# The numerator and denominator products of an mLSTM head, one at a time between the matmuls of the next large product

## The chip, the cores and the metric

One core of a Trainium2 chip runs one launch of the kernel. The metric is the device time of a launch in microseconds, as the median of several runs; before the change it is 1035.16 us, in three runs between 1034.41 and 1039.77.

## What is computed

One step of a decoder layer for T = 560 tokens: 16 meta tokens, 512 prompt tokens and 8 sequences of 4 sample tokens that carry states of their own. The layer is half a SwiGLU FFN, a mixer, and half a second FFN. The mixer sends the normalised input through one matrix `w_in` and gives parts of the result to four mLSTM heads (128 wide) and to an RG-LRU (512 channels). What the change touches is one line pair of an mLSTM head:

```
def mlstm_chunk(q, k, v, ig, logf, C0, n0, m0):
    ...
    s = jnp.einsum('bhtd,bhsd->bhts', q, k) * w_intra
    num = jnp.einsum('bhts,bhse->bhte', s, v) + w_inter[..., None] * jnp.einsum('bhed,bhtd->bhte', C0, q)
    den = jnp.sum(s, axis=-1) + w_inter * jnp.einsum('bhd,bhtd->bht', n0, q)
    h = num / jnp.maximum(jnp.abs(den), jnp.exp(-m))[..., None]
```

The prompt is one sequence and starts from zero states, so `C0` and `n0` matter for the 32 sample tokens alone.

## The kernel before

**Large products.** Weights and inputs of the matrix products are split into a high and a low part (`whi`, `wlo`, `xh`, `xl`), and a product is three passes over these, by `split_mm` (L275). A row block of `w_in` (128 output rows) takes 8 blocks of the inner dimension x 3 passes = 24 pairs of matmuls, each of a pair over half of the tokens (280, or 272 where the meta tokens aren't needed). Weights come by DMA on SP's queue, ScalarE makes the high part (L256) and VectorE the low one (L261), some blocks ahead of the products.

**The mixer's order.** The table `PLAN` (L33) lists every step of the mixer by hand: `k2` is the product of w_in for the keys of head 2, `v1` for the values of head 1, `x`, `y` and `o` for the RG-LRU's input, its output gate and the heads' output gates. TensorE, ScalarE and VectorE each run their instructions in the order in which these steps issue them. GpSimd and SP are placed by the scheduler. A row of `PLAN` begins with a large product, and the steps behind it in the row issue small work that is meant to run under or right after it.

**The steps around the change.** `n` (do_n, L1319) is the change's step: 18 products into PSUM tiles `pn` (two banks) and `pden` (one). Eight are products of `c0` (the sample states) with `qw`, 4 columns each; one is the sample's own `V5`; five are the blocks of V with the causal weights `W` (512, 400, 272, 144 and 16 columns); two small ones add up the sample's denominators; two go into `pden`. All but the last two are in full fp32, and one of those shows as two records in the profile. `cn` (L1341) copies `pn` and `pden` out on ScalarE; `cm` splits squares on ScalarE and VectorE (L1352 to L1355); `f` (L1362) sums these on TensorE; `cf` makes the reciprocal root (`rs` on ScalarE, L1370) and a Newton step on VectorE (`nt`, `rs`, L318 to L320).

`a` and `b` (lru_gate, L1043) are gate products of the RG-LRU, 6 matmuls of 292 columns each into `prg`, from `xch` and `xcl`, the split of the convolved input (`hx`, L1039 and L1040); `ta` and `tb` (L1053) are the tanh that ScalarE takes of them. `ca` and `cb` go on from there. `tv` and `tk` (turn, L1193) turn values and keys on TensorE (`pt`). `ev`, `ey` and others (L857) copy a large product out of PSUM on VectorE, with the norm's factor `r`. `hd` (L1166, L1167) splits `D`, which GpSimd sums from `W`. `p` (L1380) makes the new states, and `cp` adds them into `c0` on VectorE (L1397, `c<-c,px`).

**PSUM.** Large products, `prg`, `pn`, the `px` of step `p` and the `pv` of step `f` take turns in three tiles of two banks each (`mm_tile`). A matmul that opens a tile waits until the last reader of what lay there is done.

Lines are those of the kernel before.

Of the kernel before, what the change touches and what calls it, by code (L numbers as in the profile page):

```python
# [5 lines left out]
F32 = mybir.dt.float32  # L6
# [5 lines left out]
P = 128  # L12
KD = 8            # 1024 / 128
KF = 22           # 2816 / 128
T = 560           # 16 meta + 512 prompt + 8 x 4 sample tokens
C16 = 16
TQ = T - C16      # tokens whose outputs are needed
NP = 528
Q = 280           # half of the tokens
AHEAD = 8, 6, 5, 4          # how far loads, sums and both steps of the split run ahead of the products  # L20
MANUAL = {mybir.EngineType.PE, mybir.EngineType.Activation, mybir.EngineType.DVE}
TCUT = 272        # where the last row blocks are cut
DED = 7           # row blocks of h with a place of their own
PLAIN = 4, 3      # row blocks of h from plain products, in both FFNs
FT = 15           # where the last row blocks of h are cut for w_down
TAIL = 5          # row blocks of x that FFN 2 ends with
NB = 8
# [4 lines left out]
# the mixer, in the order of its steps (see there)  # L32
# [9 lines left out]
v1 sd0 ev1 hq1 L1 hx1 cb0 hd0 qw0 vm0 n0 a1 cc0 sk0 b1 cd0 cn0 ta1 cm0 tb1  # L42
k2 ca1 cb1 ek2 cc1 tv1 am1
x2 f0 cv1 p0 ex2 cf0 tk1 cp0 cx2 ck1
q2 L2 s1 w1 m1 sd1 eq2 hx2 hq2
v2 ev2 cd1 hd1 a2 ta2 ca2 b2 cb2 vm1 sk1 qw1 tb2 n1 cc2 cn1 hk2 ce0
x3 cm1 ex3 f1 cf1 ce1 am2
k3 w2 tv2 cx3
q3 cv2 ek3 hx3 eq3 p1 s2 tk2 cd2 cp1 ck2
v3 qw2 m2 vm2 L3 a3 sd2 hd2 ev3 n2 ta3 ca3 b3 hk3 cb3 cn2 tv3 tb3 cc3 sk2 am3 cd3  # L50
o0 p2 hq3 cv3 cm2 ce2 ce3 w3 eo0
y0 cp2 qw3 to0 ln lr ey0 gy0
o1 eo1 mo0 s3 my0 m3 f2 sd3
y1 tk3 cf2 to1 hd3 ey1 gy1 ck3 so0 mo1 n3 sk3 cn3 cm3
y2 ey2 so1 f3
o2 my1 cf3 gy2 sy0 vm3
# [11 lines left out]
IN = [t for t in PLAN if t == "g" or t[0] in "kqvoxy" and t[1].isdigit()]       # row blocks of w_in  # L68
OUT = (4, 5, 6, 7, 0, 1, 2, 3)                                   # rows of w_out
# [5 lines left out]
# the beginnings of both FFNs, in the order of their steps (see `ffn`)  # L75
# [10 lines left out]
# columns of the constant array  # L86
G1, GM, G2, GF = 0, 8, 16, 24
CW = 32           # [ct, 4]
# [6 lines left out]
CS = 72           # [ct, b, 3]  # L95
H0 = 168          # [ct, b]
N0 = 200          # [h, b]
NCONST = 232

# Products of h with w_down (see `ffn`): of its second part, and under them the first part is made in quarters,  # L100
# with their sums; then the seven products of every pair of row blocks, and between them some of the others.
# [15 lines left out]
# The seven products: weights, right side, bank, and whether they open it. After one, what its bank holds goes  # L117
# into a quarter of the result.
# [6 lines left out]
# packed columns of the causal weights of one head, by block of keys  # L125
WO = (0, 512, 912, 1184, 1328, 1344)
WTOT = 1376
T0 = (16, 128, 256, 384, 512)      # first query of each block of keys
KROWS = (128, 128, 128, 128, 16, 32)

# columns of the output array of small states
# [5 lines left out]
def hymba_step(ctx, tc, xT, wgu1, wdn1, win, wout, wgu2, wdn2, consts, small, c0t, wrg,  # L137
# [11 lines left out]
    # ---------------------------------------------------------------- weights  # L149
    # Products take their weights in the order of this list, 512 columns at a time: blocks of w, or  # L150
    # quarters and sums of quarters of [gate, up] (see ups7). Loads and splits run ahead of them.
# [19 lines left out]
    def blocks(ff):  # L171
        """Row blocks of h: the plain ones, those that go through w_down by seven products, the others, and these
        in two parts."""
        a, b = PLAIN[ff], PLAIN[ff] + 8
        return (0, a), (a, b), {"d": (b, KF), "e": (b, FT), "t": (FT, KF)}
# [30 lines left out]
    state = {"use": 0}  # L206
# [22 lines left out]
    def quarter_sum(q, k):  # L229
        """s1 = w21 + w22, s2 = s1 - w11, s3 = w11 - w21, s4 = w12 - s2, the last in place of s2."""  # L230
        if k in q:
            return
        q[k] = q["s2"] if k == "s4" else sp.tile([P, 512], F32, tag="s", name=k, bufs=4)
        x, y, op = {"s1": ("21", "22", ALU.add), "s2": ("s1", "11", ALU.subtract),
                    "s3": ("11", "21", ALU.subtract), "s4": ("12", "s2", ALU.subtract)}[k]
        dve.tensor_tensor(q[k], q[x], q[y], op=op)  # L236

    def sums(i):
# [3 lines left out]
        b = units[i - 1 - AHEAD[1] + AHEAD[3]]           # s2 is split by now  # L242
# [32 lines left out]
    def split_mm(ps, ks, xh, xl, c0, first=True, last=True, hfs=(0, 1), w=None):  # L275
        """ps += w.T @ x[k] over the k of ks, in three passes of split operands."""
        n = (T - c0) // 2
        for j, k in enumerate(ks):
# [5 lines left out]
            for i, (a, b) in enumerate(((wh, xh), (wh, xl), (wl, xh))):  # L284
                for hf in hfs:
                    state["mm"] = pe.matmul(ps[:, hf, :n], a[:, ws], b[k][:, c0 + hf * n:c0 + hf * n + n],  # L286
                                            start=first and j == 0 and i == 0,
                                            stop=last and j == len(ks) - 1 and i == 2)

# [9 lines left out]
    # -------------------------------------------------------------- constants  # L299
# [16 lines left out]
    def newton(r, v, t, c=0.0):  # L316
        """One Newton step of r towards 1/sqrt(v + c)."""
# [4 lines left out]
    def rsqrt(r, v, t):  # L322
        """r = 1/sqrt(v + eps): the table's value and a Newton step."""
# [9 lines left out]
    def ars(_=0):  # L333
        """Loads the table of 1/sqrt before it is needed."""
        act.activation(dum, eps_c, AF.Abs_reciprocal_sqrt, bias=eps_c, scale=0.0)

    class Norm:
        """Splits x*g for the products and gathers the mean square beside them."""
# [49 lines left out]
    # -------------------------------------------------------------------- FFN  # L388
    # Seven products (Strassen's, in Winograd's form) of quarters of weights x quarters of a right side
    # (halves of its rows x halves of the tokens), for two row blocks of the result at a time. The last two  # L390
    # products of a pair lie behind the first of the next.
# [12 lines left out]
    def ups7(fs, c0, zs, h, xs):  # L404
        """Row blocks of silu(gate) * up: as they are where zs has a place for them, else split into h."""
# [50 lines left out]
    def down7(c0, xs):  # L456
        """Steps of the products for row blocks d and d + 4 of what the first part of h adds to x."""
# [19 lines left out]
    def h_tiles(hp, a, b, x0):  # L477
        """Tiles of h from a to b: where x was, from slot x0, and then in this pool."""
# [16 lines left out]
    def ffn(ff, nrm, c0, hp, plan, mid, steps):  # L495
        """The first row blocks come from plain products, of x * g, and go through w_down at once; under them
        the normalised x is made in quarters (halves of the rows, halves of the tokens), with the sums of
        quarters that the seven products take. down(c, h): the products of the other chunks with w_down."""
# [106 lines left out]
    # ------------------------------------------------------- FFN 1, from DRAM  # L605
# [55 lines left out]
    def start_add(d):         # on two engines: 0 to 4, 5 to 7, and both  # L661
# [5 lines left out]
    def start_warm():         # nothing reads it: the clock of the products wakes up  # L667
# [7 lines left out]
    with tc.tile_pool(name="hp1", bufs=1) as hp, tc.tile_pool(name="sp1", bufs=1) as sp:  # L675
# [9 lines left out]
        def lru_consts():  # L685
            """softplus(-lambda) = max(-lambda, 0) + log1p(exp(-|lambda|)), and halves of what goes into tanh."""
# [12 lines left out]
    # ------------------------------------------------------------------ mixer  # L699
# [4 lines left out]
    # ------------------------------------------------- FFN 2 and the last norm  # L704
    with tc.tile_pool(name="hp2", bufs=1) as hp, tc.tile_pool(name="sp2", bufs=1) as sp:
# [4 lines left out]
        def out_square(d, a, b):  # L710
            """Squares of the tokens from a to b; x becomes x*g."""
# [23 lines left out]
        # the last row blocks in two pieces of tokens, so that the first goes out under the second  # L735
# [32 lines left out]
def mixer(ctx, tc, e):  # L768
# [23 lines left out]
    # ------------------------------------------------------------- constants  # L792
# [4 lines left out]
    cmask = mp.tile([P, P], F32, name="cmask")           # 0 where t >= s  # L797
# [3 lines left out]
    smask = mp.tile([32, NB, 4], F32, name="smask")      # same sequence and t >= s  # L801
# [5 lines left out]
    seqm = mp.tile([96, NB], F32, name="seqm")           # 1 where the row is of sequence b  # L807
# [7 lines left out]
    keep = row("keep")                                   # 0 where a sequence or a block starts  # L815
# [21 lines left out]
    # -------------------------------------------------------------- products  # L837
# [24 lines left out]
    # ----------------------------------------------------------------- gates  # L862
    # Their 8 columns stand beside the rest of their split, so that two passes do.
# [21 lines left out]
    def do_ga(_):             # ig and the forget gate's, with biases  # L885
# [17 lines left out]
    def seq(ap, j):           # column j of every sample sequence  # L903
# [26 lines left out]
    rows = dp.tile([3, H, TQ], F32, name="rows")         # of every head, to be read back on every partition  # L930
# [17 lines left out]
    # Rows to be columns: Bc at 0 (own blocks of keys), the states' weights at 32, at 64 the sums to the next  # L948
    # block and three times the sample's weights, at 96 those to the blocks after it and the sample's Bc.
# [23 lines left out]
    wst = mp.tile([P, 6, H], F32, name="wst")            # weights of the states: 4 blocks, tail, sample  # L973
# [10 lines left out]
    def do_gq(_):  # L984
# [7 lines left out]
        wsp = mp.tile([96, H], F32R, name="wsp")         # split: hi, hi, lo  # L992
# [5 lines left out]
    def bias(i, j, h):  # L998
        """Of the keys of block i for the queries of block j; 4: tail, 5: sample."""
# [535 lines left out]
```

## Time and profile before

| | |
|---|---|
| median of the runs | 1035.16 us |
| profiled execution: span from first to last instruction | 1033.8 us |
| profiled execution: a time of its own beside the span | none is given |
| TensorE busy | 1012.8 us |
| VectorE, ScalarE, GpSimd busy | 834.7, 559.9, 124.0 us |
| DMA | 99.57 MB, a mean of 96 GB/s |
| mean granted TensorE clock | 0.989 of full speed |

A row of the timeline gives the start, the length in microseconds, the engine, the line, the operation, what it writes and reads, and how many instructions were drawn together; in brackets stands how long the engine was idle before it, and who released it. A row of the waits gives who waited for whom, the total, the count and the longest. A row by windows gives a stretch and its length, then the busy time (and count) of TensorE, its weight loads, VectorE, ScalarE and GpSimd, then the granted clock, the DMA engines' share and GB/s.

### The profile page before, as it was taken

Reading aid. Unit: us, or ns where it says so; the run is one execution under the profiler, and the core shown is the slowest. Engines: PE = TensorE matmul, PEld = TensorE weight load, DVE = VectorE, ACT = ScalarE, POOL = GpSimd, SP = SyncE. Lnnn points to the kernel's source line nnn. Section 1 sums busy time; section 2 is a strip of 40 time slices with the busy share of each in tenths; the row PEclk is TensorE's granted clock in tenths of the full one; section 3 lists DMA queues with packets and bytes.
Section 4 is the critical chain, followed back from the end, with each engine's and each line's share of the span. In section 5 each row is a group of like instructions: output and inputs, shape, how many; then the busy total and the mean of one; then the engine's idle time right before and its main releaser. Section 6 shows DMA issues by size and latency. Waiting matters only on the chain.

```text
span 1033.8 us, 20127 instructions
## 1 busy us (share of the span) xinstructions
PE 1012.8 (98%) x7782; PEld 996.4 (96%) x7782; DVE 834.7 (81%) x1448; ACT 559.9 (54%) x1070; POOL 124.0 (12%) x185
## 2 busy tenths in 40 slices
PE   7999999999999999999999999999999999999995
PEld 7999999999999999989999999999999999999995
DVE  7889888888778797888868775789888889859774
ACT  5544555566554455466756643554555566644542
POOL 2000000000000034444443101100000000000114
PEclk9999999999999999999999999999999999999998
DMA  6322322322332334223132123122332323233222
GB/s 215 103 83 72 110 86 101 104 93 96 101 100 64 92 109 143 86 79 127 48 120 85 62 92 119 58 67 101 103 103 95 110 93 112 92 102 93 82 65 87
DMA packets 57479, 99.57 MB, mean 96 GB/s; under 512 B 7840, under 2 KB 14624, under 8 KB 57384
## 3 DMA queue, kind: packets, MB, share of 16 engines
q1 hardware_dynamic: 57384, 98.30, 29.1%
q8 instruction: 61, 1.00, 0.4%
q14 instruction: 34, 0.28, 0.1%
HBM read 93.57 MB, written 4.70 MB: 95 GB/s over the span
## 4 chain that ended last, share of the span: by engine, by line
PE 86%; DVE 7%; issue 2%; ACT 1%; POOL 1%; DMA 1%; SPq 0%; POOLq 0%; DVEq 0%; ACTq 0%
PE pb L397 26%; PE pad L397 20%; PE pd L286 15%; PE po L286 7%; PE pu L286 4%; PE pg L286 4%; PE pv L286 2%; PE py L286 2%; DVE wlo L261 1%; PE pn L1328 1%; PE pd L753 1%; PE p L286 1%; PE px L286 1%; PE pk L286 1%; PE pn L1324 0%
## 5 line engine op out<-in xcount | busy, mean ns | idle before, releaser
L256 ACT CAST whi<-raw 128x512 fp32r<-128x512 f32 (+2 forms) x289 | 173.6, 608 | 176.0 <-PE pad L397 41.1
L261 DVE TENSOR_TENSOR wlo<-raw,whi 128x512 fp32r<-128x512 f32 (+2 forms) x289 | 197.1, 699 | 69.3 <-ACT whi L256 68.9
L256 ACT CAST whi<-s 128x512 fp32r<-128x512 f32 x180 | 112.1, 623 | 105.8 <-PE pb L397 36.4
L261 DVE TENSOR_TENSOR wlo<-s,whi 128x512 fp32r<-128x512 f32 x180 | 124.2, 691 | 12.8 <-ACT whi L256 6.5
L397 PE MATMUL pad<-q21h,whi 128*128 128x280 f32 (+1 forms) x360 | 104.2, 289 | 0.9 <-ACT whi L256 0.9
L397 PE MATMUL pb<-qt4l,whi 128*128 128x280 f32 (+1 forms) x360 | 104.0, 289 | 0.0
L397 PE MATMUL pad<-q21l,whi 128*128 128x280 f32 (+1 forms) x360 | 104.0, 289 | 0.0
L397 PE MATMUL pad<-q21h,wlo 128*128 128x280 f32 (+1 forms) x360 | 104.0, 289 | 0.0
L397 PE MATMUL pb<-qt4h,whi 128*128 128x280 f32 (+1 forms) x360 | 103.9, 289 | 0.0
L397 PE MATMUL pb<-qt4h,wlo 128*128 128x280 f32 (+1 forms) x360 | 103.9, 289 | 0.0
L366 POOL TENSOR_TENSOR acc<-acc,sq 128x560 f32<-128x560 f32 (+1 forms) x12 | 18.1, 1512 | 435.1 <-ACT sq L365 434.8
L397 PEld LDWEIGHTS pad<-q21h,whi 128*128 128x128 f32 x360 | 67.8, 188 | 1.1 <-ACT whi L256 1.1
L397 PEld LDWEIGHTS pb<-qt4h,whi 128*128 128x128 f32 x360 | 67.9, 189 | 0.0
L397 PEld LDWEIGHTS pb<-qt4h,wlo 128*128 128x128 f32 x360 | 67.8, 188 | 0.0
L397 PEld LDWEIGHTS pad<-q21l,whi 128*128 128x128 f32 x360 | 67.8, 188 | 0.0
L397 PEld LDWEIGHTS pb<-qt4l,whi 128*128 128x128 f32 x360 | 67.8, 188 | 0.0
L397 PEld LDWEIGHTS pad<-q21h,wlo 128*128 128x128 f32 x360 | 67.8, 188 | 0.0
L236 DVE TENSOR_TENSOR s<-raw 128x512 f32<-128x512 f32 x90 | 61.5, 683 | 1.7 <-DMA raw<-in_wdn 1.7
L286 PE MATMUL pd<-hl,whi 128*128 128x280 f32 (+1 forms) x294 | 61.6, 291 | 0.8 <-DVE hl L529 0.8
L286 PE MATMUL pd<-hh,whi 128*128 128x280 f32 (+1 forms) x294 | 61.3, 290 | 0.8 <-ACT hh L526 0.8
L286 PE MATMUL pd<-hh,wlo 128*128 128x280 f32 (+1 forms) x294 | 61.3, 289 | 0.0
L721 POOL TENSOR_TENSOR acc<-acc,sq 128x272 f32<-128x272 f32 x12 | 11.4, 969 | 350.4 <-ACT sq L717 350.4
(457 smaller groups left out, 3029.0 us busy)
## 6 DMA issues: line engine op xcount, KB each, us to landing
raw<-in_wgu SPq DMA_DIRECT2D x174, 256.0 KB, 2.7
raw<-in_wdn SPq DMA_DIRECT2D x71, 256.0 KB, 2.8
raw<-in_win SPq DMA_DIRECT2D x50, 256.0 KB, 2.8
raw<-in_wout SPq DMA_DIRECT2D x16, 256.0 KB, 2.7
raw<-in_wdn SPq DMA_DIRECT2D x18, 192.0 KB, 2.4
out_y<-X SPq DMA_DIRECT2D x4, 544.0 KB, 3.1
c<-in_c0t SPq DMA_DIRECT2D x4, 512.0 KB, 3.6
out_o_cs<-c SPq DMA_DIRECT2D x4, 512.0 KB, 3.9
```

Of the source, the lines that this page charges most:

```text
L236: dve.tensor_tensor(q[k], q[x], q[y], op=op)
L256: act.copy(ready[i][0][:, :src.shape[-1]], src)
L261: dve.tensor_tensor(lo, src, hi, op=ALU.subtract)
L286: state["mm"] = pe.matmul(ps[:, hf, :n], a[:, ws], b[k][:, c0 + hf * n:c0 + hf * n + n], start=first and j == 0 and i == 0, stop=last and ...
L366: (dve if d == KD - 1 else pool).tensor_tensor(self.acc[:, c0:], self.acc[:, c0:], s[:, c0:], op=ALU.add)
L397: pe.matmul(ps, a[:, k * P:k * P + P], b, start=first and k == 0 and i == 0, stop=k == KD // 2 - 1 and i == 2, skip_group_check=not first)
L721: pool.tensor_tensor(acc[:, a:b], acc[:, a:b], s[:, :b - a], op=ALU.add)
L753: pe.matmul(ps, u[:, i % 4 * P:i % 4 * P + P], v[:, C16 + a:C16 + b], start=i == 0 and m == 0, stop=f == c1 - 1 and m == 2)
L1328: pe.matmul(pn[:, 0, a:512], V[:KROWS[i], i, :P], W[:KROWS[i], WO[i]:WO[i] + 512 - a], start=i == 0, stop=i == 4)
```

## The change

`do_n` no longer issues its products. It appends 18 closures to a list. `split_mm` calls `fill()` after every pair of matmuls, which takes one closure from the list and issues it. A new step `nz`, directly behind the large product, issues what is left (nothing, as 18 is less than 24). Inside a head's group the order is new: each block of V is followed by two products of `c0`, then V5 and the rest.

```
-    state = {"use": 0}
+    state = {"use": 0, "fill": []}
+
+    def fill(n=1):
+
+        for _ in range(min(n, len(state["fill"]))):
+            state["fill"].pop(0)()
...
                     state["mm"] = pe.matmul(ps[:, hf, :n], a[:, ws], b[k][:, c0 + hf * n:c0 + hf * n + n],
                                             start=first and j == 0 and i == 0,
                                             stop=last and j == len(ks) - 1 and i == 2)
+                fill()
...
         pn, pd = ps["n", h] = mm_tile("pn"), aux_tile("pden")
-        for b in range(NB):
-            pe.matmul(pn[:, 1, 4 * b:4 * b + 4], d["c0"][:, b, :], d["qw"][:, b, :], start=b == 0, stop=False)
-        pe.matmul(pn[:, 1, 0:32], d["V5"], W[:32, WO[5]:WO[5] + 32], start=False, stop=True)
+        fill = e["state"]["fill"]
+
+        def mm(*a, **k):
+            fill.append(lambda: pe.matmul(*a, **k))
         for i in range(5):
             a = T0[i] - C16
...
+            mm(pn[:, 0, a:512], V[:KROWS[i], i, :P], W[:KROWS[i], WO[i]:WO[i] + 512 - a], start=i == 0, stop=i == 4)
+            for b in range(2 * i, min(2 * i + 2, NB)):
+                mm(pn[:, 1, 4 * b:4 * b + 4], d["c0"][:, b, :], d["qw"][:, b, :], start=b == 0, stop=False)
...
+    steps["nz"] = lambda _: e["fill"](99)
```

`PLAN` changes with it. `n0` goes behind a1 and b1 and its products run in k2; `n1` goes to the end of its row and runs in x3; `n2` goes behind a3, b3 and tv3 and runs in o0; `n3`, behind tk3 as before, runs in y2. `cn` and `cm` follow the large product. `f1` goes from before k3 to after it, `f3` from before o2 to after it. For example, of the row of v1 and the next:

```
-v1 sd0 ev1 hq1 L1 hx1 cb0 hd0 qw0 vm0 n0 a1 cc0 sk0 b1 cd0 cn0 ta1 cm0 tb1
-k2 ca1 cb1 ek2 cc1 tv1 am1
...
+v1 sd0 ev1 hq1 L1 hx1 cb0 hd0 qw0 vm0 a1 cc0 sk0 b1 cd0 ta1 tb1 n0
+k2 nz ca1 cn0 cb1 ek2 cm0 cc1 tv1 am1
```

The rest of the diff takes comments out. What it does to the engines' order shows at two places. The first is TensorE around head 0's group. `pv` is the product v1, `prg` the gates of step a1, `pk` the product k2. Before, v1 is followed by the group, and the group by a1:

```order
L286 MATMUL pv<-xh_5039,wlo 128x280 x2
L1324 MATMUL pn<-qw,c_5533 128x4 x8
L1325 MATMUL pn<-W,V_5682 128x32
L1328 MATMUL pn<-W,V 128x512
L1328 MATMUL pn<-W,V 128x400
L1328 MATMUL pn<-W,V 128x272
L1328 MATMUL pn<-W,V 128x144
L1328 MATMUL pn<-W,V 128x16
L1330 MATMUL pn<-W,ones_84 128x32
L1331 MATMUL pn<-qn,ones_84 128x32
L1333 MATMUL pden<-zh,ones_r_5089 128x512
L1049 MATMUL prg<-xch,wrgh_5576 128x292
```

After, a1 follows v1:

```order
L291 MATMUL pv<-xh_5039,whi 128x280 x2
L291 MATMUL pv<-xl_5040,whi 128x280 x2
L291 MATMUL pv<-xh_5039,wlo 128x280 x2
L1055 MATMUL prg<-xch,wrgh_5576 128x292
L1055 MATMUL prg<-xcl,wrgh_5576 128x292
L1055 MATMUL prg<-xch,wrgl_5577 128x292
```

And at the start of k2, on the same engine:

```order
L1055 MATMUL prg<-xch,wrgl_5104 128x292
L291 MATMUL pk<-xh_4558,whi 128x280 x2
L1332 MATMUL pn<-W,V 128x512
L291 MATMUL pk<-xl_4559,whi 128x280 x2
L1332 MATMUL pn<-qw,c_5533 128x4
L291 MATMUL pk<-xh_4558,wlo 128x280 x2
```

The gate products of a1 and b1 moved ahead of the whole group, and the group moved into k2. (Lines of the kernel after are 5 to 11 higher here; L1332 is the one line that issues all products of the group.) The second place is ScalarE around head 2's group: `th<-prg` is the tanh of the gates, of a3 first and of b3 last, and `hn<-pn` and what follows is `cn2`, which copies head 2's group out. Before:

```order
L1166 CAST zh<-kT 128x512
L1073 ACT_TABLE_LOAD
L1073 ACTIVATE th<-tt 128x584
L1341 COPY hn<-pn 128x512
L1342 COPY hn<-pn 128x32
L1343 ACTIVATE dd<-pn 128x32
L1344 ACTIVATE dd<-pden 128x512
L1345 ACTIVATE sq<-hn 128x544
L1053 ACT_TABLE_LOAD
L1053 ACTIVATE th<-prg,lc 128x584
```

After:

```order
L1172 CAST zh<-kT 128x512
L1079 ACT_TABLE_LOAD
L1079 ACTIVATE th<-tt 128x584
L1059 ACT_TABLE_LOAD
L1059 ACTIVATE th<-prg,lc 128x584
L261 CAST whi<-raw 128x512 x2
L1352 COPY hn<-pn 128x512
```

The second tanh moved ahead of the copies out of `pn`, directly behind the second table load; the first table load and what stands before it stayed. On TensorE, the product o0 with the group of head 2 comes behind a3, b3 and tv3, and the tile `pn` of this group takes the banks in which b3's gates lay.

More of the change, by code (lines that the diff above doesn't have):

```diff
@@ L41 @@
 q1 a0 eq1 w0 b0 ta0 s0 m0 cx1 tk0 tb0 ck0 ca0
-v1 sd0 ev1 hq1 L1 hx1 cb0 hd0 qw0 vm0 n0 a1 cc0 sk0 b1 cd0 cn0 ta1 cm0 tb1
-k2 ca1 cb1 ek2 cc1 tv1 am1
+v1 sd0 ev1 hq1 L1 hx1 cb0 hd0 qw0 vm0 a1 cc0 sk0 b1 cd0 ta1 tb1 n0
+k2 nz ca1 cn0 cb1 ek2 cm0 cc1 tv1 am1
 x2 f0 cv1 p0 ex2 cf0 tk1 cp0 cx2 ck1
 q2 L2 s1 w1 m1 sd1 eq2 hx2 hq2
-v2 ev2 cd1 hd1 a2 ta2 ca2 b2 cb2 vm1 sk1 qw1 tb2 n1 cc2 cn1 hk2 ce0
-x3 cm1 ex3 f1 cf1 ce1 am2
-k3 w2 tv2 cx3
+v2 ev2 cd1 hd1 a2 ta2 ca2 b2 cb2 vm1 sk1 qw1 tb2 cc2 hk2 ce0 n1
+x3 nz cn1 ex3 cm1 ce1 am2
+k3 f1 cf1 w2 tv2 cx3
 q3 cv2 ek3 hx3 eq3 p1 s2 tk2 cd2 cp1 ck2
-v3 qw2 m2 vm2 L3 a3 sd2 hd2 ev3 n2 ta3 ca3 b3 hk3 cb3 cn2 tv3 tb3 cc3 sk2 am3 cd3
-o0 p2 hq3 cv3 cm2 ce2 ce3 w3 eo0
+v3 qw2 m2 vm2 L3 a3 sd2 hd2 ev3 ta3 ca3 b3 hk3 cb3 tv3 tb3 cc3 sk2 am3 cd3 n2
+o0 nz cn2 p2 hq3 cv3 cm2 ce2 ce3 w3 eo0
 y0 cp2 qw3 to0 ln lr ey0 gy0
 o1 eo1 mo0 s3 my0 m3 f2 sd3
-y1 tk3 cf2 to1 hd3 ey1 gy1 ck3 so0 mo1 n3 sk3 cn3 cm3
-y2 ey2 so1 f3
-o2 my1 cf3 gy2 sy0 vm3
+y1 tk3 cf2 to1 hd3 ey1 gy1 ck3 so0 mo1 sk3 n3
+y2 nz cn3 ey2 cm3 so1
+o2 f3 my1 cf3 gy2 sy0 vm3
 y3 sy1 ey3 my2 eo2 gy3 my3
@@ L1322, in do_n @@
         pn, pd = ps["n", h] = mm_tile("pn"), aux_tile("pden")
-        for b in range(NB):
-            pe.matmul(pn[:, 1, 4 * b:4 * b + 4], d["c0"][:, b, :], d["qw"][:, b, :], start=b == 0, stop=False)
-        pe.matmul(pn[:, 1, 0:32], d["V5"], W[:32, WO[5]:WO[5] + 32], start=False, stop=True)
+        fill = e["state"]["fill"]
+        def mm(*a, **k):
+            fill.append(lambda: pe.matmul(*a, **k))
         for i in range(5):
             a = T0[i] - C16
-            pe.matmul(pn[:, 0, a:512], V[:KROWS[i], i, :P], W[:KROWS[i], WO[i]:WO[i] + 512 - a],
-                      start=i == 0, stop=i == 4)
-        pe.matmul(pn[:, 1, 64:96], one_m[1][:32, :], W[:32, WO[5]:WO[5] + 32], start=True, stop=False)
-        pe.matmul(pn[:, 1, 64:96], one_m[1], d["qn"].rearrange("p b j -> p (b j)"), start=False, stop=True)
+            mm(pn[:, 0, a:512], V[:KROWS[i], i, :P], W[:KROWS[i], WO[i]:WO[i] + 512 - a], start=i == 0, stop=i == 4)
+            for b in range(2 * i, min(2 * i + 2, NB)):
+                mm(pn[:, 1, 4 * b:4 * b + 4], d["c0"][:, b, :], d["qw"][:, b, :], start=b == 0, stop=False)
+        mm(pn[:, 1, 0:32], d["V5"], W[:32, WO[5]:WO[5] + 32], start=False, stop=True)
+        mm(pn[:, 1, 64:96], one_m[1][:32, :], W[:32, WO[5]:WO[5] + 32], start=True, stop=False)
+        mm(pn[:, 1, 64:96], one_m[1], d["qn"].rearrange("p b j -> p (b j)"), start=False, stop=True)
         for i, x in enumerate(d["Ss"]):
-            pe.matmul(pd, ones_r[1], x, start=i == 0, stop=i == 1)
+            mm(pd, ones_r[1], x, start=i == 0, stop=i == 1)
+    steps["nz"] = lambda _: e["fill"](99)
     @step
```

## The prediction

> **What bounds the kernel now.** I read the page first, then TensorE's waits, then the timeline of TensorE around the four places of the small products, and the granted clock there.
>
> ```profile
> span 1033.8 us, 20127 instructions
> ...
> PE 1012.8 (98%) x7782; PEld 996.4 (96%) x7782; DVE 834.7 (81%) x1448; ACT 559.9 (54%) x1070; POOL 124.0 (12%) x185
> ...
> PE 86%; DVE 7%; issue 2%; ACT 1%; POOL 1%; DMA 1%; SPq 0%; POOLq 0%; DVEq 0%; ACTq 0%
> ...
> PE po L286 <- DVE c L1397: 0.7, 1, 0.7
> ```
>
> TensorE is busy for 98% of the span and is 86% of the chain that ended last. The last row is the longest wait that TensorE has inside the mixer. So nothing can be won by filling holes of TensorE there: there are none. The small products could only become cheaper, and the timeline says how much. These rows give, for each head, the first eight products (`c0` x `qw`) and what follows the group; the sixth row ends head 1's x3, which follows its group:
>
> ```profile
> 452.00 1.85 PE L1324 MATMUL pn<-qw,c 128*128 128x4 f32 x16
> ...
> 459.52 0.29 PE L1049 MATMUL prg<-xch,wrgh 128*128 128x292 f32 x1
> ...
> 493.54 1.84 PE L1324 MATMUL pn<-qw,c 128*128 128x4 f32 x16
> ...
> 501.12 0.42 PE L286 MATMUL px<-xh,whi 128*128 128x280 f32 x2
> ...
> 507.33 0.29 PE L1362 MATMUL pv<-sqh,ones_r 128*128 128x272 f32 x1
> ...
> 533.40 1.84 PE L1324 MATMUL pn<-qw,c 128*128 128x4 f32 x16
> ...
> 539.30 0.30 PE L1049 MATMUL prg<-xch,wrgh 128*128 128x292 f32 x1
> ...
> 572.29 1.85 PE L1324 MATMUL pn<-qw,c 128*128 128x4 f32 x16
> ...
> 579.88 0.41 PE L286 MATMUL py<-xh,whi 128*128 128x272 f32 x2
> ```
>
> The same 18 products take 459.52 - 452.00 = 7.52 us for head 0, 7.58 for head 1, 5.90 for head 2 and 7.59 for head 3. The eight 4-column products at its start cost 1.84 us everywhere, so the difference lies in what comes behind them. The view by windows says why (columns: window and its length, then busy time and count of PE, PEld, DVE, ACT, POOL, then the granted TensorE clock):
>
> ```profile
> 455.05:458.46 3.41, 3.41 (x10) 2.22 (x8) 3.38 (x3) 0.00 (x0) 1.67 (x1) 0.50 0.47 137
> 496.00:499.40 3.40, 3.40 (x6) 1.66 (x5) 3.40 (x4) 3.36 (x4) 3.40 (x3) 0.50 0.00 0
> 533.40:539.30 5.90, 5.90 (x37) 4.72 (x36) 2.95 (x5) 5.76 (x8) 3.06 (x4) 1.00 0.06 21
> 574.40:577.90 3.50, 3.50 (x6) 1.75 (x6) 1.73 (x4) 2.54 (x6) 2.24 (x1) 0.52 0.02 5
> ```
>
> In three heads of four the clock stands at half for about 3.4 us, beginning 2 to 3 us after the start of the 4-column products. TensorE shows as busy, yet those 1.84 us move hardly any columns. So there is something to win: (7.52 + 7.58 + 7.59) - 3 x 5.90 = 4.99 us, 0.48% of the run. (About 0.5%, 5.2 us, is what a measurement of this kernel can tell from no change.)
>
> **What the change adds to TensorE's own work: nothing that I can price.** 18 products per head stay 18 products; each is put behind a pair of large matmuls. Head 1's x3 takes 507.33 - 501.12 = 6.21 us for 48 matmuls, 129 ns each; a record of a 4-column product takes 1.84/16 = 115 ns. If each matmul takes the longer of its own time and the next weight load, a pair of large ones plus one small product costs the same alone as mixed. The one place where full-precision products already stand between split ones:
>
> ```profile
> 524.12 0.29 PE L1279 MATMUL pA<-qT,kT 128*16 128x16 f32 x4
> 524.35 0.40 PE L1282 MATMUL pB<-zh 128*128 128x272 f32 x1
> ```
>
> Four records in 0.23 us, both changes of type included, is less than four records of the 4-column products: no price of its own for changing between the two. I take 0 for mixing; the gain side is a rival below.
>
> **What it takes away: the cover.** In before, the 6 to 7.5 us of each group stand where VectorE and ScalarE have to catch up. The change moves the next gate products and the turns in front of the group, and the group itself into a large product whose PSUM bank is read by someone else first. Head by head, with the time at which the last producer ends:
>
> Head 0. a1 now follows v1 at once, at 452.00. Its second matmul needs `xcl`, which VectorE makes behind `vT` (and `vT` needs v1's end):
>
> ```profile
> 452.20 0.74 DVE L857 TENSOR_TENSOR vT<-pv,r 128x560 f32<-128x560 f32 x1 [0.29 <-PE pv L286]
> ...
> 453.45 0.82 DVE L1040 TENSOR_TENSOR xcl<-xc,xch 128x584 fp32r<-128x584 f32 x1
> ...
> 506.23 0.71 DVE L1353 TENSOR_TENSOR sql<-sq,sqh 128x544 fp32r<-128x544 f32 x1
> ```
>
> It is ready at 454.27, one matmul (0.13 us) after 452.00: a stall of 2.1 us. k2 with n0 in it then runs at full speed, which recovers 1.6. cm0 now stands after k2 on VectorE: its two operations (the last row is one of them, in head 1; two are 1.42 us) come ahead of what tk1's bank waits for; between 0 and 1.4, I take 1.1. Sum: 2.1 - 1.6 + 1.1 = **+1.6 us**.
>
> Head 1. n1 runs in x3: 1.7 us recovered, so x3 ends at 493.54 + 1.6 + 6.21 + 5.90 = 507.25. But f1 moves from before k3 to after it, and with it everything that follows on VectorE up to the sum into `c`, on which v3's bank depends:
>
> ```profile
> 514.03 0.49 PE L1199 MATMUL pt<-ident,vT 128*128 128x128 f32 x3
> ...
> 509.06 0.66 ACT L1370 ACTIVATE rs<-dd 128x544 f32<-128x544 f32 x1 [2.43 <-DVE dd L1369]
> ...
> 509.75:526.25 16.50, 16.20 (x124) 15.15 (x122) 15.57 (x19) 10.17 (x30) 4.24 (x12) 1.00 0.24 80
> ...
> 510.67 2.31 DVE L319 SCALAR_TENSOR_TENSOR nt<-nt,rs 128x544 f32<-128x544 f32 x1
> ...
> 514.48 1.29 DVE L261 TENSOR_TENSOR wlo<-raw,whi 128x512 fp32r<-128x512 f32 x2
> ...
> 526.28 0.53 PE L286 MATMUL pv<-xh,whi 128*128 128x280 f32 x2 [0.33 <-DVE c L1397]
> ```
>
> From f1's start (507.33) to the first operation behind `rs` (509.72) it is 2.4 us; f1 and k3 together take 514.03 - 507.33 = 6.7, k3 alone, of x3's size, 6.2. After the change f1 starts at 507.25 + 6.2 = 513.45, so that operation starts at 515.85. VectorE is busy for 15.57 of the 16.5 us from there to v3's start, which waits for `c`; of this only the two `wlo` (1.29) now come earlier. So `c` ends at 515.85 + 14.3 = 530.2, and v3, which started at 526.28, starts **3.9 us later than before** (head 0's 1.6 included). The 2.31 us row is three times as long as its like; at 0.7 us the sum is 2.3. I take 3.9, as the same work on GpSimd runs beside it.
>
> Head 2. n2's first product goes to the bank of b3's gates, and waits until ScalarE has read them (the `th` at the end of these rows):
>
> ```profile
> 533.47 0.62 ACT L1166 CAST zh<-D 128x512 fp32r<-128x512 f32 x1 [3.42 <-POOL D L1307]
> 533.99 0.74 ACT L1053 ACTIVATE th<-prg,lc 128x584 f32<-128x584 f32 x1
> ...
> 536.94 1.28 ACT L1073 ACT_TABLE_LOAD   x1
> 538.24 0.69 ACT L1073 ACTIVATE th<-tt 128x584 f32<-128x584 f32 x1
> 538.94 0.59 ACT L1341 COPY hn<-pn 128x512 f32<-128x512 f32 x1
> ...
> 540.77 1.28 ACT L1053 ACT_TABLE_LOAD   x1
> 542.06 0.75 ACT L1053 ACTIVATE th<-prg,lc 128x584 f32<-128x584 f32 x1
> ...
> 540.67 0.50 PE L286 MATMUL po<-xh,whi 128*128 128x272 f32 x2
> ```
>
> Without the copies out of `pn` between them, the second table load follows at 538.93, and that `th` ends at 538.93 + 1.28 + 0.75 = 540.96, which is 7.5 us after `zh<-D` begins. `D` comes from GpSimd after the weights that VectorE makes behind `c`, so the chain moves by the same 3.9 as v3. On TensorE, b3 and tv3 take 540.67 - 539.30 = 1.37 us after a3's end (533.40), then o0's first pair 2 x 0.13. So TensorE stands still for 540.96 - 533.40 - 1.37 - 0.26 = 5.9 us, wherever in it the parts lie (tv3 waits for `vT` in the same stretch). There was no lost clock to recover: **+5.9 us**. Queued behind that waiting matmul is all of o0.
>
> Head 3. n3's first product takes the bank of y1, so it waits for `yg`, which VectorE makes late:
>
> ```profile
> 574.79 0.71 DVE L857 TENSOR_TENSOR yg<-py,r 128x544 f32<-128x544 f32 x1
> ```
>
> y2 starts where n3 did, at 572.29, and its first pair ends at 572.55; `yg` ends at 575.50: a stall of 3.0, less 1.7 of recovered clock, **+1.3 us**, or -1.7 if VectorE, held up less by then, has caught up. The wait of o1 for `c` (0.7, the row at the start) should go, as `c` gains time in head 2: **-0.7**.
>
> Sum: 3.9 + 5.9 + 1.3 - 0.7 = +10.4 us.
>
> **The clock after the new holes.** Half clock costs 4.99/3 = 1.7 us each time. It came after 2 us of hardly any columns, but not each time: head 2's identical group escaped. [...] I take one: +1.7. The total is +12.1 us, on the span of 1033.8; the page gives no other time for the profiled execution. The median of the runs is 1035.16, so I put it there: 1035.16 + 12.1 = **1047.3 us**. [...]
>
> **The rivals.**
> 1. *The clean gain.* VectorE and ScalarE, whose work is the same, follow TensorE's new order: xcl, `th` and `yg` come in time, all three half-clock stretches vanish, the wait of 0.7 goes too: 1035.16 - 5.0 - 0.7 = 1029.5 us. It decides if the bank of n2's first product is free within 0.26 us of o0's start. Against it: the 7.5 us of ScalarE's chain, in fixed order. Chance 0.08.
> 2. *The cancelling.* Stalls come, but the engines behind use each one to catch up, so that only head 2's (5.9) is left in full, against 5.0 + 0.7 gained, with up to 3 us for head 0: 1033 to 1040. Chance 0.12.
> 3. *The mixed weight loads hide.* If loads run several matmuls ahead, those of the 4-column products vanish under large matmuls: at most 4 x 1.84 = 7.4 us less, 1047.3 - 7.4 = 1039.9. Against it: 115 ns per record in a row of them, beside 129 for a large one, leaves 14 ns of room per matmul. Chance 0.06. [...]
> 4. *Every hole halves the clock.* The holes of heads 0 and 3 bring it too, 2 x 1.7 more, and the rest as forecast: 1050.7, up to 1053. Chance 0.17.
>
> That the change isn't carried out is no rival: the order shows the products between the pairs.
>
> **How the numbers follow.** The forecast (1041 to 1049: its low end is 10.4 less 1.6 for head 1's short row and 3.0 for head 3, 1041.0) has 0.57. Range: from 1037, inside the cases of cancelling and hiding, to 1052, inside that of the clock: what is left out is the clean gain, half of the cancelling and a few hundredths above, about 0.18. Chances: faster 0.08 (the clean gain), within 0.5% (1030.0 to 1040.3) the cancelling and the hiding, less what of them ends higher, 0.16, slower 0.76.
>
> **What would show it.** In the profile after: a wait of PE for ACT `th` at n2's first product of several us, one for DVE `xcl` at a1 of about 2, one for DVE `yg` in y2 of about 3, v3 starting near 530; granted clock 1.00 through k2 and x3, 0.50 after head 2's hole. The forecast is wrong if TensorE's waits in the mixer stay under 3 us in all, or if o0 with n2 takes less than 13 us, or if mixed pairs run slower or faster than 0.26 us plus the small product's own time.

## The result and the profile after

The changed kernel takes 1053.54 us (median of 4 runs, 1051.54 to 1056.47) against 1035.84 us before: 1.0159 times as long, with an interval of [1.0137, 1.0182]. It is slower, as forecast, and 1.5 us beyond the upper end of the forecast's range. (Two runs further down, one of experiment 4 with 2531.73 us and one of experiment 9 with 3260.53 us, took far longer than the others of their kernel and are left out of the medians.) The profiled execution has a span of 1050.2 us against 1033.8, 16.4 more. The page after:

```profile
span 1050.2 us, 20122 instructions
...
PE 1014.7 (97%) x7782; PEld 997.1 (95%) x7782; DVE 829.9 (79%) x1448; ACT 558.6 (53%) x1070; POOL 121.3 (12%) x185
```

The counts are the same; the busy time of TensorE grew by 1.9 us, the rest of the 16.4 us is time in which it stood. The waits of TensorE (who waited for whom, total, times, longest), those of the mixer alone:

```profile
PE pn L1332 <- ACT th L1059: 5.0, 2, 4.6
...
PE pn L1332 <- DVE yg L863: 2.8, 1, 2.8
PE prg L1055 <- DVE xcl L1046: 2.0, 1, 2.0
...
PE px L1391 <- ACT V L1224: 1.5, 1, 1.5
PE pv L291 <- DVE c L1408: 1.4, 1, 1.4
PE pt L1205 <- DVE xp L1027: 1.3, 1, 1.3
...
PE pt L1205 <- DVE vT L863: 0.5, 1, 0.5
```

That is 14.5 us, where before had the 0.7 for `c` at o1 (gone) and 0.3 for `c` at v3: 13.5 us more. The places are those that the forecast named: b3's tanh at head 2's first product, `yg` at head 3's, `xcl` at a1, `xp` at tk1, `V` and `c` behind f1's move. The granted clock of the kernel after, in two stretches by windows:

```profile
456.00:459.40 3.40, 3.40 (x14) 2.86 (x12) 3.33 (x5) 2.00 (x3) 0.19 (x1) 0.51 0.43 125
548.10:551.50 3.40, 3.35 (x10) 2.32 (x10) 3.37 (x5) 0.50 (x1) 1.21 (x2) 0.50 0.00 0
```

The timeline of the kernel after around head 1's mixed product x3 (start, length):

```profile
498.56 0.43 PE L291 MATMUL px<-xh,whi 128*128 128x280 f32 x2
499.39 1.13 PE L1332 MATMUL pn<-W,V 128*128 128x512 f32 x2 [0.40 <-ACT th L1059]
...
505.78 0.50 PE L291 MATMUL px<-xh,wlo 128*128 128x280 f32 x2
506.12 0.28 PE L1332 MATMUL pn<-qw,c 128*128 128x4 f32 x2
506.26 0.50 PE L291 MATMUL px<-xh,whi 128*128 128x280 f32 x2
506.69 0.39 PE L1332 MATMUL pn<-W,V 16*128 16x16 f32 x2
507.01 0.52 PE L291 MATMUL px<-xl,whi 128*128 128x280 f32 x2
507.46 0.40 PE L1332 MATMUL pn<-W,V 32*128 32x32 f32 x2
507.80 0.52 PE L291 MATMUL px<-xh,wlo 128*128 128x280 f32 x2
...
511.68 0.42 PE L291 MATMUL pk<-xh,whi 128*128 128x280 f32 x2
```

Two readings. First, the clock fell twice, not once: behind the hole at a1 (456.0) and behind the one at head 2 (548.1), 1.7 us each, against three times before. Second, x3 with its group took 511.68 - 498.56 - 0.40 = 12.7 us at full clock, not 6.21 + 5.90 = 12.1. The rows show where: a pair of large matmuls with one 4-column product takes 506.26 - 505.78 = 0.48 us, of which the pair alone is 0.26; a pair with a product over 16 or 32 rows takes 507.01 - 506.26 = 0.75 and 507.80 - 507.01 = 0.79. (For y2 with head 3's group, the other one at full clock, it is 602.24 - 586.74 - 2.84 = 12.7 us against 6.0 + 5.9.)

So the 16.4 us are: 13.5 of waits, 2.4 of mixing (4 x 0.6, taken from x3), less 1.6 of clock (5.0 lost before, 3.4 after), and 1.0 ahead of the first group: 15.3. The last is no effect of the change: v1 ends at 452.00 in the profile before and at 453.01 in this one, and in ten other profiles with the same program up to there it lies between 451.7 and 453.7. Of the remaining 1.1 us, 0.2 is the wait of q3 for `dd`; the rest I can't assign.

### The profile page after: what moved, and what is told of

The parts are those of the page before. It is cut to its first block, busy times and chain, and to the rows that moved or that the text cites. A ratio compares the mean times of both kernels' runs of the same rounds, so it can differ in the third digit from the quotient of the medians.

```text
span 1050.2 us, 20122 instructions
## 1 busy us (share of the span) xinstructions
PE 1014.7 (97%) x7782; PEld 997.1 (95%) x7782; DVE 829.9 (79%) x1448; ACT 558.6 (53%) x1070; POOL 121.3 (12%) x185
## 4 chain that ended last, share of the span: by engine, by line
PE 88%; DVE 4%; ACT 3%; issue 2%; POOL 2%; DMA 1%; SPq 0%; POOLq 0%; ACTq 0%; DVEq 0%
PE pb L403 26%; PE pad L403 19%; PE pd L291 14%; PE po L291 7%; PE pu L291 3%; PE pg L291 3%; PE pn L1332 2%; PE pv L291 2%; PE pk L291 2%; PE py L291 2%; PE px L291 1%; PE pd L759 1%; PE p L291 1%; PE pq L291 1%; DVE wlo L266 1%
## 5 line engine op out<-in xcount | busy, mean ns | idle before, releaser
L403 PE MATMUL pb<-q11h,whi 128*128 128x280 f32 (+1 forms) x180 | 52.4, 291 | 0.0
```

The costliest lines, as they stand in the source:

```text
L403: pe.matmul(ps, a[:, k * P:k * P + P], b, start=first and k == 0 and i == 0, stop=k == KD // 2 - 1 and i == 2, skip_group_check=not first)
```

## The experiments

The theory going in: the loss is the lost cover, that is, waits for VectorE and ScalarE that the groups used to hide, with half-clock stretches behind the holes and a small price of mixing. The main rival: the products simply cost more between large matmuls. Each run was timed beside the kernel before on the same chip; ratios are to that.

**1. Only the inner order.** The place stays; V and 4-column products alternate:

```
         for i in range(5):
             pe.matmul(pn[:, 0, a:512], V[:KROWS[i], i, :P], ...)
+            for b in range(2 * i, min(2 * i + 2, NB)):
+                pe.matmul(pn[:, 1, 4 * b:4 * b + 4], d["c0"][:, b, :], d["qw"][:, b, :], ...)
```

> The kernel before, with one edit: inside the group the blocks of V alternate with the 4-column products (each block of V, then two of them), the group stays where it was. Theory of the clock (three half-clock stretches come from 1.84 us of 4-column products in a row): no such row is left, granted clock 1.00 through all four groups, each 5.9 us, the whole about 5.0 us faster than before (near 1031). Rival (the half clock comes from the group's full-precision products as such, or from their weight loads): three or four stretches stay and the time is the same within 1 us. If alternating has a price of its own, a group is longer than 5.9 us at full clock.

Measured: 0.9987 [0.9975, 0.9999], 1034.73 against 1036.25 us; span 1032.0. The windows of its four groups:

```profile
452.50:459.70 7.20, 7.20 (x49) 6.21 (x48) 6.94 (x8) 3.42 (x9) 3.47 (x3) 1.00 0.51 151
493.40:499.00 5.60, 5.60 (x36) 4.63 (x35) 5.10 (x6) 5.52 (x7) 4.13 (x6) 1.00 0.21 71
533.40:539.00 5.60, 5.60 (x37) 4.61 (x36) 2.76 (x5) 5.52 (x8) 1.91 (x3) 1.00 0.01 2
572.40:578.00 5.60, 5.60 (x36) 4.61 (x35) 3.77 (x7) 4.97 (x10) 1.42 (x1) 1.00 0.02 5
```

Its waits:

```profile
PE pv L1362 <- DVE sql L1353: 1.5, 1, 1.5
PE pt L1199 <- DVE xp L1021: 1.3, 1, 1.3
PE po L286 <- DVE c L1397: 1.1, 1, 1.1
```

In the first table the clock stands at 1.00 in all four groups of this execution. That the half clock of before came from the 4-column products standing in a row is not shown by it. The same order, issued in a row, stands in experiments 2, 8 and 9, and there five of twelve groups end in half clock with TensorE busy, as in head 1 of experiment 2, head 3 of experiment 8 and head 2 of experiment 9:

```profile
503.60:507.00 3.40, 3.40 (x16) 3.29 (x15) 3.25 (x5) 2.68 (x6) 1.13 (x2) 0.50 0.03 5
...
582.81:586.21 3.40, 3.40 (x15) 3.20 (x15) 3.40 (x6) 0.48 (x1) 0.81 (x1) 0.50 0.00 0
...
544.01:547.41 3.40, 3.40 (x16) 3.11 (x15) 2.30 (x2) 3.17 (x6) 1.83 (x2) 0.50 0.00 0
```

Nor was the clock much higher over the runs: its mean was 0.988 to 0.995 in the twelve of this experiment, with a median of 0.991, and 0.986 to 0.993 in the seventeen of the kernel before beside them, with the same median. The execution shown is one of three with 0.995. So the rival of the expectation, that the group's full-precision products as such bring the half clock, isn't excluded.

In the executions shown, each group takes 5.6 us, so 7.52 + 7.58 + 5.90 + 7.59 - 4 x 5.6 = 6.2 us are won there. The span shows 1.8 of it, and 0.5 is lost ahead of the groups, where v1 ends later. Two waits of 1.5 and 1.3 us are new and those for `c` (at o1 and v3) are 0.7 longer: over half of the gain was given back at once. The expectation, 5.0 us faster, took the gain for the result and missed that.

**2. The group in a row at the new place.** All of the change, except that step `n` issues its products at once, ahead of the large product:

```
             mm(pd, ones_r[1], x, start=i == 0, stop=i == 1)
+        e["fill"](99)
```

> The kernel after, with the group issued in a row where step n now stands (behind the gate products and turns, ahead of the large product) instead of between pairs. Theory of the lost cover: the order of everything else is that of after, so the waits for xcl (2.0), th (about 4.9), yg (about 3.1), V and c stay, only the price of mixing (0.6 us per head) goes: 2.4 us under after, 1050 to 1052. Rival (mixing itself is the cost, the waits follow from it): 1036 to 1040, with waits of TensorE in the mixer under 4 us in all.

Measured: 1.0057 [1.0038, 1.0075], 1042.34 us, 11 under the changed kernel. Both expectations missed: it is too fast for "the waits stay", and too slow, with 7.8 us of waits, for "mixing is the cost". Its waits:

```profile
PE pt L1205 <- DVE xp L1027: 2.2, 1, 2.2
PE prg L1055 <- DVE xcl L1046: 2.0, 1, 2.0
PE px L1392 <- ACT V L1224: 1.5, 1, 1.5
PE pv L291 <- DVE c L1409: 1.4, 1, 1.4
```

Its timeline at head 2's group:

```profile
542.89 1.02 PE L1332 MATMUL pn<-W,V 128*128 128x512 f32 x2
...
548.88 0.66 PE L291 MATMUL po<-xh,whi 128*128 128x272 f32 x2
```

The order of everything else is that of after, yet the waits for the gates' tanh (5.0, of which 4.6 for b3's) and for `yg` (2.8) are gone, because in a row the group and the large product open their PSUM tiles 6 us apart. A mixed group needs its tile while the large product's is open. Of three tiles that is one more than was free: at head 2 the turn of tv3 holds one (its `pt` comes from the same three), o0 takes the one of a3's gates, and the group needs that of b3's. The mixing also costs more than the 0.6 per head taken from the old order: the alternating row takes 5.6, so mixed it is 12.7 - 6.2 - 5.6 = 0.9 per head more.

**3. The group opens its tile first.** A product of the group ahead of each pair instead of behind it:

```
+                fill()
                 for hf in hfs:
                     state["mm"] = pe.matmul(...)
-                fill()
```

> The kernel after, with each product of the group ahead of its pair instead of behind it, so that the group opens its PSUM tile before the large product does. Theory of the two open tiles: the group gets the bank that comes free first and the large product the other, whose reader is the same late one; the wait stands at the large product's first matmul, same size within 0.5 us, the time within 2 us of after. Rival (it only matters which of the banks the group got): the waits of 4.6 and 2.8 us vanish, 7 us or more under after.

Measured: 1.0148 [1.0121, 1.0176], 1052.43 us; the interval overlaps with that of after. Its waits:

```profile
PE po L292 <- ACT th L1059: 3.7, 1, 3.7
PE py L292 <- DVE yg L863: 2.3, 1, 2.3
```

The same two readers are waited for, now by the large products `po` and `py`; with the wait for `vT`, 0.5 after and 1.7 here, head 2 stands still for 5.4 us here and 5.2 there. So it isn't which bank the group got; it is that two have to be free at once.

**4. Mixing from the 17th pair on**, three products after each pair:

```
-                fill()
+                if j * 3 + i >= 16:
+                    fill(3)
```

> The kernel after, with the products of the group mixed in only from the 17th pair of the large product on, three after each pair. Theory of the two open tiles (a mixed group needs its own PSUM tile while the large product's is open, so the banks of both last readers must be free at once): 16 pairs or 4.1 us later the wait for th at head 2 is 0.5 or less, those for yg and for th at head 1 are gone, 7.5 us less waiting, 1044 to 1046 (xcl, V and c stay). Rival (ScalarE and VectorE are late by more than that and the wait only moves): waits of 2 us or more remain in o0 and y2, 1049 or more.

Measured: 1.0071 [1.0044, 1.0099], 1043.99 us, at the lower end of what was expected. Its waits:

```profile
PE pt L1206 <- DVE xp L1028: 2.7, 1, 2.7
PE prg L1056 <- DVE xcl L1047: 2.0, 1, 2.0
PE px L1392 <- ACT V L1225: 1.5, 1, 1.5
PE pn L1333 <- ACT th L1060: 1.4, 1, 1.4
```

4.1 us later, `yg` is no longer waited for, and of the two waits for tanh 1.4 us are left (0.5 was expected); that for `xp` rose from 1.3 to 2.7. x3 with its group took 11.9 us here: three small products behind one pair leave no price of mixing.

**5. Only the products of full height mixed**; the 16-row block of V, V5, the sums and `pden` follow the large product:

```
-    def fill(n=1):
+    def fill(n=1, all=False):
...
-        for _ in range(min(n, len(state["fill"]))):
+        for _ in range(min(n, len(state["fill"]) - (0 if all else state.get("hold", 0)))):
...
+        e["state"]["hold"] = 6
...
-    steps["nz"] = lambda _: e["fill"](99)
+    steps["nz"] = lambda _: e["fill"](99, True)
```

> The kernel after, with the last six products of a group (the 16-row block of V, V5 and the sums, and pden) in a row directly behind the large product instead of between its pairs; the first twelve stay mixed. Theory (mixing has a price, and the products with 16 and 32 rows carry it, 0.5 us each between pairs against 0.25 to 0.3 in a row): a large product with its group at full clock without waits takes about 12.0 us instead of 12.7, about 2.5 us under after in all, the waits for th, yg, xcl unchanged. Rival (the price is in the 4-column products or in every change of weights): it stays at 12.5 or more.

Measured: 1.0188 [1.0161, 1.0216], 1056.11 us. The interval overlaps with that of after, so nothing was gained, but the term in question came out as expected: x3 starts at 500.31 and k3 at 512.24, without a wait between, by its timeline:

```profile
500.31 0.43 PE L291 MATMUL px<-xh,whi 128*128 128x280 f32 x2
...
512.24 0.42 PE L291 MATMUL pk<-xh,whi 128*128 128x280 f32 x2
```

And by windows, two stretches of it:

```profile
529.20:536.80 7.60, 7.60 (x34) 6.35 (x34) 4.56 (x6) 1.54 (x7) 1.69 (x7) 0.55 0.63 190
594.30:601.20 6.90, 6.23 (x19) 4.54 (x19) 4.25 (x8) 2.56 (x7) 0.00 (x0) 0.51 0.04 14
```

11.9 us instead of 12.7: the price of mixing sits in the products with few rows. What took the gain away in this execution, the slowest of the four, is the clock: stretches at half clock of 7 us, not 3.4, behind holes of the same size (the wait for `yg`, 2.8 us, at 594.3), and one behind the wait for V. The wait for `xp` is also longer, 3.0 us instead of 1.3.

**6. Head 0's hole closed**: `xcl` made before the copy of v1.

```
-v1 sd0 ev1 hq1 L1 hx1 cb0 ...
+v1 sd0 hx1 ev1 hq1 L1 cb0 ...
```

> The kernel after, with the split of head 0's gate input (hx1) ahead of the copy of v1 out of PSUM (ev1) on ScalarE and VectorE, so that xcl no longer stands behind vT. Theory: the hole of 2.0 us at a1 goes, and with it the half-clock stretch behind it (1.7 us): 3.7 us under after. Rival (the half clock there has another cause, and VectorE's later work only moves): the hole goes but the clock still falls within 4 us of it, or the 2 us come back at the next wait, 0 to 2 us under after.

Measured: 1.0174 [1.0154, 1.0195], 1054.15 us: nothing gained. Its timeline at head 0:

```profile
452.98 0.40 PE L1055 MATMUL prg<-xcl,wrgh 128*128 128x292 f32 x1 [0.36 <-DVE xcl L1046]
...
456.48 0.70 PE L1332 MATMUL pn<-W,V 128*128 128x512 f32 x1 [1.49 <-ACT th L1059]
```

A stretch of it at head 3, by windows:

```profile
588.40:595.40 7.00, 6.82 (x23) 5.12 (x23) 3.77 (x8) 2.50 (x6) 0.00 (x0) 0.52 0.12 38
```

Of the hole of 2.04 us, 1.49 came back 3.5 us later as a wait for a tanh at head 0's own first product; this part of the rival is right. The clock did not fall there any more, but at head 3 it now did, for 7 us, behind a hole of 2.86 us. In the kernel after no half clock followed the same hole (2.84); the next section shows how the two lay.

**7. Head 2's group one product later**, in y0:

```
-o0 nz cn2 p2 hq3 cv3 cm2 ce2 ce3 w3 eo0
-y0 cp2 qw3 ...
+o0 p2 hq3 cv3 ce2 ce3 w3 eo0 n2
+y0 nz cn2 cm2 cp2 qw3 ...
```

> The kernel after, with the group of head 2 one large product later (mixed into y0 instead of o0; its copies and squares follow y0). Theory: the wait for b3's tanh (4.6 us) and the half-clock stretch behind it (1.7 us) go, 5 to 6.5 us under after, unless y0's bank brings a wait of its own. Rival (VectorE and ScalarE behind set the pace there, the hole only moves): a wait of 3 us or more shows at y0, o1 or head 3, and the time stays within 2 us of after.

Measured: 1.0253 [1.0234, 1.0272], 1062.84 us, 9 slower than after. Its waits:

```profile
PE pn L1332 <- DVE og L863: 4.5, 1, 4.5
PE po L291 <- DVE c L1408: 3.1, 1, 3.1
```

The rival's case: the second open tile now waits for `og`, the copy of o0, and with cm2 and cp2 pushed back, o1 waits for `c`. A later product does not help, since each large product is preceded by one whose copy is still to come.

**8. Head 1 undone**, on the kernel of experiment 2: its group, cn1 and f1 at the places of before.

```
-... tb2 cc2 hk2 ce0 n1
-x3 nz cn1 ex3 cm1 ce1 am2
-k3 f1 cf1 w2 tv2 cx3
+... tb2 n1 cc2 cn1 hk2 ce0
+x3 cm1 ex3 f1 cf1 ce1 am2
+k3 w2 tv2 cx3
```

> The kernel after with the groups issued in a row at the new places, and for head 1 the order of before (its group ahead of x3 as before, f1 ahead of k3 again). Theory (f1 behind k3 makes ScalarE late for V and VectorE late for c): the waits for V (1.5) and for c before v3 (1.36) go, that for sql before f1 comes (up to 1.5), 1 to 2.5 us under the kernel with groups in a row at the new places. Rival (they come from the load of head 0 before): both stay.

Measured: 1.0029 [1.0015, 1.0042], 1039.96 us, 2.4 under experiment 2. The wait for V is gone, that for `c` before v3 is 0.7 instead of 1.4. The wait for `sql` that was expected to come in their place did not. So the change at head 1 is what made these two; the edit undoes the group's place and f1's together, and which of them did it is not shown.

**9. and 10. Towards a better kernel.** From experiment 1, whose waits are VectorE's. Three steps moved back whole:

```
-k2 ca1 cb1 ek2 cc1 tv1 am1
-x2 f0 cv1 p0 ex2 cf0 tk1 ...
+k2 ca1 cb1 ek2 tv1 am1
+x2 f0 cv1 p0 ex2 cc1 cf0 tk1 ...
```

(and cc2 behind cm1, cm2 behind cp2 alike).

> The kernel before with the inner order of the group changed (V alternating with the 4-column products), and three pieces of VectorE's work moved behind what TensorE waits for: cc1 behind ex2, cc2 behind cm1, cm2 behind cp2. Theory (the 5 us of clock were given back as waits for xp 1.3, sql 1.5 and c 0.7 and 1.1, because the shorter groups cover less): these waits shrink to under 1.5 us in all, 3 us under the kernel with the inner order alone, 1031 to 1032. Rival (VectorE is loaded there; what is moved back makes the next wait): waits of 3 us or more at other places, time unchanged against that kernel.

Measured: 1.0031 [1.0018, 1.0044], 1040.08 us, slower than before. The waits that were aimed at went, and these came:

```profile
PE pq L286 <- DVE dd L1369: 2.8, 1, 2.8
PE pv L286 <- DVE c L1397: 1.8, 1, 1.8
PE px L1380 <- ACT V L1218: 1.7, 1, 1.7
```

The five operations of cc1, put ahead of cf0's, made those late. Then only the last operation of cc1 and cc2, before which VectorE stands idle for GpSimd:

```
+        if ct not in (1, 2):
+            do_cz(ct)
+
+    @step
+    def do_cz(ct):
+        a0 = L[ct]["a0"]
         dve.tensor_scalar(a0, a0, -2.0, -1.0, op0=ALU.mult, op1=ALU.add)
...
+x2 f0 cv1 p0 ex2 cz1 cf0 tk1 ...
+x3 cm1 cz2 ex3 f1 cf1 ...
```

> The kernel before with the inner order of the group changed, and on VectorE only the last operation of cc1 and cc2 (the one that stands 1.35 us idle for GpSimd) moved behind ex2 and cm1, and cm2 behind cp2. Theory (the 5 us of clock and 1.2 us of shorter groups were given back as waits of TensorE for VectorE, of which 2.7 us are VectorE's own idle time in cc): the waits for xp, for sql and for c before o1 fall to under 1.3 us in all, 2.5 to 3.5 us under the kernel with the inner order alone, about 1031.5, 0.4% faster than before. Rival (VectorE's load, not that wait, makes it late): within 1 us of the kernel with the inner order alone.

Measured: 0.9976 [0.9965, 0.9987], 1033.36 against 1035.76 us: faster than both kernels, by 2.4 us against before. The waits for `xp` and `sql` shrank to 0.8 and 1.0, that for `c` at o1 went, that for `c` at v3 grew to 1.0; the three left are 2.8 us. Of those aimed at, `xp` and `sql` still make 1.8 us, where under 1.3 was expected. Against experiment 1 this is 1.1 us by ratio; the intervals overlap, the rival had said within 1 us, and the median of the clock over the runs is higher here too (0.9935 against 0.991). So the step back of the last operation is not shown to have won time.

## Why the prediction was off, point by point

**The sign, the places and the waits were right.** Forecast against measured, for each hole: `xcl` 2.1 and 2.0; tk1 1.1 and 1.3; head 2 (tv3 and tanh together) 5.9 and 5.2; `yg` 3.0 and 2.8; the late start of v3 2.3 more in head 1 (3.9 less head 0's 1.6), and measured 533.80 - 526.28 - 5.0 = 2.5, where 5.0 is by how much a2 was late (491.94 before, 496.97 after). That last agreement is in part luck: the waits on the way were 3.1 us longer than before instead of 4.0, and the mixing that the forecast left out (0.6) stands in for most of the rest. Nor did the forecast have p1's wait for V, which is 1.5 of the 3.1. The wait of 0.7 at o1 went, as said. The order and the rows of before were enough for all this. That the mixing of two open tiles is behind the two largest was said only in half: the forecast named the bank, but put part of the loss on the group's move ahead of which gates and turns run. Experiments 2 and 3 show that the second open tile alone makes 7.8 us of waits.

**The step that failed is the clock after the new holes: "I take one".** Two came in the profiled execution, and that is the one of four runs with the highest mean clock (0.992; the others had 0.990, 0.987 and 0.984, and the last two took 3 to 5 us longer). Head 0's account (2.1 - 1.6 + 1.1) took the 1.6 us of before's half clock as recovered, though the hole of 2.1 us itself stood in its place; measured, head 0 cost 5.0 - 1.0 = 4.0 us instead of 1.6. That there would be exactly one is shown by no run: the rows of before give the price, 1.7 us, but TensorE has no hole of this size in the mixer there. The runs showed two here, and half clock behind 20 of 24 holes of 2 us or more. Some evidence was there: half clock followed 1.84 us of few columns three times in four, so a hole of 2.1 us should have been given the same odds. Over the profiles with this hole (after, and experiments 2, 3, 4, 5, 7 and 8), half clock followed it in six of seven. The rival "every hole halves the clock" had 0.17, and its 1050.7 us came nearer, though only two of the three holes brought it here.

**The second mis-sized term is the price of mixing: 0 forecast, 0.6 us per head measured, 2.4 in all.** The row of 16-column products that was to show it (four records in 0.23 us) has products over all 128 rows, next to each other, so it did not hold what matters: a product of few rows alone between two of 128 rows. Experiment 5 shows that these carry it. Mixed pairs that run slower than their parts were one of the forecast's own signs of being wrong.

The sum by kinds, on the span: the forecast's waits were 15.4 us (12.1 with 5.0 of recovered clock added and 1.7 of new half clock taken off) and measured 13.5; clock -3.3 and measured -1.6; mixing 0 and 2.4. That makes 14.3 instead of 12.1; with the 1.0 ahead of the groups and the 1.1 left over it is the 16.4 measured. The medians differ by 17.7, 1.3 more than the two spans.

**The rivals.** The clean gain did not come. What it counted on can happen, as the profile of experiment 1 has none of the three half-clock stretches, but most of that is given back as waits even where no product is moved. Hiding of weight loads did not show: a pair with one 4-column product costs 0.48 us, the sum of its parts (0.26 and 2 x 0.115).

**What the traces settle of the clock, and what stays open.** The hole of 2.3 to 2.9 us at head 3 was followed by none (after), 3.4 us (experiments 3 and 7) or 7 us (experiments 5 and 6) of half clock. The cases differ in where the hole lay. In each of the twelve profiles the starts of the half-clock stretches are whole multiples of 3.413 us apart: in before, 455.07, 496.03 and 574.53 by 12 and 23 of them, in after, 455.92 and 548.08 by 27, in experiment 5, 481.80, 529.58, 550.06 and 594.44 by 14, 6 and 13. A slot is here the time from one such place to the next, counted on from these starts. The work lies differently against the slots in each execution: the hole of 2.04 us for `xcl` (453.30 to 455.34) lay in one slot in after, and half clock began at that slot's end, 455.92; in experiment 5 the same hole (454.03 to 456.07) was cut at 454.49 into 0.46 and 1.58 us, and none followed. The first two rows are the two slots that share after's hole of 2.84 us, 1.81 and 1.03 of it; the last two are from experiment 6, where one slot has 2.50 us of the hole of 2.86:

```profile
585.63:589.04 3.41, 1.60 (x14) 1.36 (x12) 3.22 (x5) 3.36 (x5) 0.00 (x0) 1.00 0.23 74
589.04:592.45 3.41, 2.38 (x13) 1.88 (x14) 1.64 (x4) 2.82 (x7) 0.00 (x0) 1.00 0.00 0
...
584.81:588.22 3.41, 0.92 (x9) 0.67 (x6) 3.31 (x6) 3.14 (x4) 0.00 (x0) 1.00 0.08 30
588.23:591.64 3.41, 3.06 (x8) 2.02 (x9) 1.65 (x4) 2.50 (x6) 0.00 (x0) 0.50 0.00 0
```

By the records of the granted clock in the twelve traces, there are between 420 and 640 us 21 slots with at least 1.97 us of holes, and half clock follows all of them. Of the 24 holes of 2 us or more there, 20 were followed by half clock, and the other four were cut so that no slot had more than 1.81 us. So a forecast from the profile before could not know the number of drops, only their odds. What counts beside holes stays open: eight drops came with no hole in the slot ahead of them (in before, TensorE is busy for all 3.41 us ahead of each of its three), each from a slot that lay mostly in a group issued in a row. That head 2 escaped in before fits a slot that began at 533.58, 0.18 us after the group, but no run here shifted a group alone against the slots.

## What to carry to other kernels

Mixing a small accumulating product into a large one needs its PSUM tile open at the same time, so count the tiles that are free at its start; a group in a row needs only one at a time, and here that took 7.8 us of waits away (experiment 2). On a tuned schedule, a stretch of one engine's work is also the cover of the others: before shortening or moving it, list what would be late next, as here both the moved group and the merely shortened one gave time back that way. And give every new hole of 2 us or more on TensorE the price of a half-clock stretch, 1.7 us for 3.4 us of it: 20 of 24 were followed by one here.

## What the runs showed of the hardware that was not expected

- A full-precision product over 16 or 32 rows costs about 0.5 us alone between pairs of 128-row matmuls (0.75 to 0.79 us for the step, less 0.26 for the pair), and x3 with its group takes 0.8 us less (11.9 against 12.7) when these stand in a row.
- The half-clock stretches of one execution began whole multiples of 3.413 us apart (12 and 23 of them in before, 27 in after), and the work lay differently against these starts in each execution. All 21 slots of that length with 1.97 us or more of holes were followed by half clock; behind the same hole of 2.04 us it came in after and not in experiment 5.
- The granted clock also fell with TensorE busy for the whole slot ahead (3.41 of 3.41 us, three times in before): in three of four groups with eight 4-column products in a row, and in five of twelve where these alternate with larger products (experiments 2, 8 and 9).
- Some half-clock stretches lasted about 7 us, others 3.4: 529.2 to 536.8 in experiment 5 and 588.4 to 595.4 in experiment 6 show mean clocks of 0.55 and 0.52.
